# An MLP of Strassen products on one core: two pieces of the second product and two feature products in turn, in place of one and one

## The chip, the core and the metric

The kernel runs on one core of a Trainium2 chip. A core has five engines that run side by side and meet through semaphores: TensorE (PE, matmuls; PEld is its weight load), VectorE (DVE), ScalarE (ACT), GpSimd (POOL) and SyncE (SP, which here only issues DMAs). The metric is the device time of the whole program in microseconds, from its first to its last instruction, as the median over several executions.

## The reference

The program is an encoder trunk of two post-norm layers over 512 tokens of width 1024. Layer 0 mixes tokens with a gated DeltaNet, layer 1 with a gated linear attention; each is followed by the same kind of MLP, which is the part that matters here:

```python
def _sq_relu_mlp(h, w1, w2):          # h: 512 x 1024, w1: 1024 x 4096, w2: 4096 x 1024
    a = jax.nn.relu(jnp.matmul(h, w1))
    return jnp.matmul(a * a, w2)

x = _layernorm(DEEPNORM_ALPHA * x + m, ln1_g[i], ln1_b[i])                           # m: the mixer's output
x = _layernorm(DEEPNORM_ALPHA * x + _sq_relu_mlp(x, mlp_w1[i], mlp_w2[i]), ln2_g[i], ln2_b[i])
```

## The kernel before

**Three matmuls for one.** Every operand is split into a high part and the rest (`split`, line 92: a ScalarE copy, line 102, and a VectorE subtraction, line 107), and each product is the sum of high by high, high by low and low by high (`mm3`, lines 125 to 130). So all matmuls of the MLP stand on lines 128, 129 and 130, and are told apart by their tiles.

**Groups.** The MLP (`mlp`, line 352) cuts the 4096 features into four groups of 1024. For each group the first product makes the squared ReLU features `h`, and the second multiplies them by 1024 rows of w2 and adds the result to the residual `xt`. Group 0 is done with plain projections. After it, three group passes (`for gi in range(G - 1)`, line 760) each run the second product of group gi together with the feature products of group gi + 1; `last` (line 603) does the second product of group 3 with the layer norm.

**Feature products.** From group 1 on, the first product is a Strassen scheme. A group has eight feature tiles, taken as four pairs (`Pair`, line 450). A pair is made by seven half-size products (`products`, line 491): each has 4 steps of 3 matmuls, with a 128 x 128 weight and 256 moving columns, 12 in all. In order they are called A to G in this document (numbers 1, 2, 6, 5, 7, 3, 4 in the code). A, C, E and G write the PSUM tile `fx`, which accumulates over them and is copied out in between; B and then D and F write the two halves of `fyz`. The weights come from `prepare` (lines 461 to 475, run for the next pair behind D: A and B share one weight tile, D has its own) and from `late` (C and G share one tile, made behind F of the pair before; E and F share another, made behind B).

**The second product** is a Strassen scheme too (`second`, line 564): seven steps, each with four pieces (`chunks`, line 544). A piece has 2 steps of 3 matmuls with 512 moving columns, 6 in all, into one of two PSUM banks of the step; the tiles are pX, pY and pZ. A step's pieces take its two w2 tiles in turn, and for each tile both banks. With its first piece a step orders the split of the next step's operands (`upto`), with its fourth the addition of both banks to `xt` on VectorE (lines 534 and 536) and the next w2 loads. The fourth and the fifth step use the same two banks.

**The order.** 28 pieces meet 28 products in a pass. `stream` (line 740) gives the products one at a time, and between them orders the loads of the next pair (behind A) and the weights named above. The loop at lines 766 to 769 takes one piece from `second` and then as many products as `k < i + 1` allows, which is one. In the third pass (m = 24) all products that are left come behind piece 23 (the pieces count from 0), so that pieces 24 to 27 follow them. `in_order` (line 60) ties TensorE's instructions to the order in which they are written, within the block that it encloses. The other engines' order, and TensorE's between blocks, is set by the planner of the framework, from dependencies, the order of writing and its own estimates.

Of the kernel before, what the change touches and what calls it, by code (L numbers as in the profile page):

```python
# [351 lines left out]
def mlp(c, w1, w2, g, b, out=None, extra=None, room=0):  # L352
# [14 lines left out]
    with c.banks(pj=2, X=2, Y=2, Z=2), tc.tile_pool(name="mlp", bufs=2) as pool:  # L367
# [51 lines left out]
        def new_h():  # L419
            return [pool.tile([P, HF, S], F32, name="h", tag="h", bufs=3) for _ in range(2)]  # L420
# [143 lines left out]
        def second(gi, h, a):  # L564

            a11, a12, a21, a22 = quarters(h)
            tags = "ZX" if gi + 2 == G else "XZ"
            X, Y, Z = banks(tags[0]), banks("Y"), None
            load(gi, 1, 0)

            def upto(i):

                if i == 5:
                    V.tensor_tensor(a21, a22, a21, ALU.subtract)
                elif i == 6:
                    V.scalar_tensor_tensor(a11, a21, -1.0, a11, ALU.mult, ALU.subtract)
                elif i == 7:
                    V.scalar_tensor_tensor(a21, a11, -1.0, a22, ALU.mult, ALU.subtract)
                elif i == 3:
                    V.scalar_tensor_tensor(a12, a12, -1.0, a11, ALU.mult, ALU.subtract)  # L580
                b = pair({2: a12, 5: a21, 6: a11, 7: a21, 3: a12, 4: a22}[i])
                split(i)
                return b

            steps = ((1, 2, 0, 0, ALU.add, None), (2, 5, 0, 0, ALU.add, None), (5, 6, 2, 1, ALU.subtract, None),
                     (6, 7, 0, 1, ALU.subtract, (0, 0)), (7, 3, 2, 1, ALU.subtract, (0, 1)),
                     (3, 4, 0, 1, ALU.subtract, (1, 1)), (4, None, 2, 0, ALU.add, None))
            for i, nx, t, hf, op, more in steps:
                if i == 2:
                    Z = banks(tags[1])  # L590
                bk = Z if i == 2 else Y if i in (5, 3) else X
                for n, _ in enumerate(chunks(bk, a, i, i in (1, 2, 5))):
                    if n == 0 and nx:
                        b = upto(nx)
                    if n == 3:
                        for j in range(2):
                            add(t + j, hf, bk[j], op)
                        if more:
                            load(gi + 1, *more)
                    yield  # L600
                a = b
# [138 lines left out]
        def stream(gi, nh):  # L740

            for p in range(GF // 2):
                i = (gi - 1) * (GF // 2) + p
                for n, _ in enumerate(ready[i].products(nh)):
                    if n == 0:
                        begin(i + 1)
                    elif n == 1:
                        ready[i].late(1, (7, 3))
                    elif n == 3:
                        prepare(i + 1)  # L750
                    elif n == 5:
                        finish(i + 1)
                    if p == 3 and n == 2 and gi + 1 == G:
                        load(gi, 1, 0, c.wst)
                    if p == 3 and n == 2:
                        split(1, None if gi + 1 < G else True)
                        stream.a = pair(quarters(nh)[0])
                    yield

        for gi in range(G - 1):  # L760
            nh = new_h()
            more = stream(gi + 1, nh)
            n, k = 28, 0
            m = 24 if gi + 2 == G else 28
            with c.in_order(mybir.EngineType.PE):
                for i, _ in enumerate(second(gi, h, a)):
                    while k < n and (k < i + 1 or i + 1 == m):
                        next(more, None)
                        k += 1
                for _ in more:  # L770
                    pass
            h, a = nh, stream.a
# [1040 lines left out]
def body(tc, nc, a, out):  # L1813
    with contextlib.ExitStack() as es:
        def pool(name, bufs, **kw):
            return es.enter_context(tc.tile_pool(name=name, bufs=bufs, **kw))

        c = Ctx(tc, nc, (pool("const", 1), pool("big", 1), pool("wst", 3), pool("whl", 3), pool("small", 4)))
        x = a["x"][0]
        gdn(c, (a["a_in"], a["a_gates"]), a["a_conv"][0], a["a_alog"][0], a["a_dt_bias"][0], a["a_norm_g"][0],  # L1820
            a["a_out"], a["ln1_g"][0], a["ln1_b"][0], x, a["xt"], a["w1_0"])
        with tc.tile_pool(name="gcst", bufs=1) as gp:
            gc = []
            mlp(c, a["w1_0"], a["w2_0"], a["ln2_g"][0], a["ln2_b"][0],
                room=32, extra=lambda tmp: gc.append(GlaConst(c, gp, a["b_gate_b"][0], a["b_norm_g"][0], tmp)))
            gla(c, gc[0], (a["b_in"], a["b_vr"], a["b_gates"]), a["b_gate_w2"][0], a["b_out"], a["ln1_g"][1], a["ln1_b"][1], a["w1_1"])
        mlp(c, a["w1_1"], a["w2_1"], a["ln2_g"][1], a["ln2_b"][1], out=out[0])
# [18 lines left out]
```

## Time and profile before

| what | us |
|---|---|
| median of 3 executions | 1327.93 (1327.3 to 1328.49) |
| the profiled execution | 1328.52 |
| its span, first to last instruction | 1326.6 |
| TensorE busy | 1307.4 |
| VectorE busy | 1107.7 |
| ScalarE busy | 805.2 |
| pieces and products in turn, first MLP | about 466 to 701 |
| the same, second MLP | about 1040 to 1275 |

In a timeline a row has the start in us, the duration in us, the engine, the line, the operation, the tile written and the tiles read (buffer numbers left out), and the size. A matmul's duration overlaps with that of the next, so the pace of TensorE is read from the distance between starts. In a table of stretches each engine has its busy time and, after an x, the number of instructions that lie in the stretch or reach into it. In a list of waits a row says who waited for whom, how long in total, how often, and the longest.

### The profile page before, as it was taken

What the parts mean: (1) busy time and instruction counts of PE and PEld (TensorE: products, weight loads), DVE (VectorE), ACT (ScalarE), POOL (GpSimd) and SP (SyncE); (2) the same over time, 40 slices, a digit from 0 to 9 for tenths busy, and PEclk for the clock granted to TensorE, in tenths of its full rate; (3) what the DMA queues carried; (4) which work ended last, traced back from release to release, by engine and by line L of the source; (5) the groups of instructions that cost most, each with busy time, mean ns of one, the idle gap of its engine ahead of it and who ended that gap; (6) DMA issues with size and microseconds to landing.
All of it is one profiled execution on the core that took longest, in us unless ns stands there. A gap on an engine that the chain in (4) does not pass through costs nothing.

```text
span 1326.6 us, 22309 instructions
## 1 busy us (share of the span) xinstructions
PE 1307.4 (99%) x8659; PEld 1113.2 (84%) x8659; DVE 1107.7 (83%) x1823; ACT 805.2 (61%) x1598; POOL 124.8 (9%) x177
## 2 busy tenths in 40 slices
PE   9999999999999999999999999999999999999996
PEld 7777877787777889999998888888889889999985
DVE  7787888888668988989988787967879789989887
ACT  4757666767643666566667754654456466666656
POOL 5000000000000910101102200000001001101021
PEclk9999999999999999999999999999999999999998
DMA  5210120211222585675648521111216465657465
GB/s 181 96 49 33 49 65 33 64 49 57 73 99 85 189 178 154 156 191 153 151 150 170 149 90 64 65 63 64 95 64 213 105 193 154 149 172 161 142 143 143
DMA packets 44045, 154.36 MB, mean 116 GB/s; under 512 B 5419, under 2 KB 5795, under 8 KB 43939
## 3 DMA queue, kind: packets, MB, share of 16 engines
q1 hardware_dynamic: 32163, 110.85, 24.9%
q0 software_dynamic: 11776, 42.08, 16.1%
q8 instruction: 68, 1.11, 0.3%
q14 instruction: 38, 0.31, 0.1%
HBM read 113.99 MB, written 2.10 MB: 88 GB/s over the span
## 4 chain that ended last, share of the span: by engine, by line
PE 92%; ACT 3%; DVE 3%; issue 1%; DVEq 0%; POOL 0%; ACTq 0%; POOLq 0%
PE fx L128 3%; PE fx L130 3%; PE fx L129 3%; PE pX L130 3%; PE pX L129 3%; PE pX L128 3%; PE pjv L128 3%; PE pjv L129 3%; PE pjv L130 3%; PE m L1708 3%; PE fyz L128 3%; PE fyz L129 3%; PE fyz L130 3%; PE pY L129 2%; PE pY L128 2%; PE pY L130 2%
## 5 line engine op out<-in xcount | busy, mean ns | idle before, releaser
L102 ACT CAST wh<-wst 128x1024 fp32r<-128x1024 f32 x152 | 159.4, 1049 | 110.3 <-PE fyz L129 35.3
L107 DVE TENSOR_TENSOR wl<-wst,wh 128x1024 fp32r<-128x1024 f32 x150 | 184.3, 1229 | 42.2 <-ACT wh L102 41.9
L107 DVE TENSOR_TENSOR w2l<-w2r,w2h 128x1024 fp32r<-128x1024 f32 x92 | 112.3, 1221 | 24.0 <-ACT w2h L102 23.8
L102 ACT CAST w2h<-w2r 128x1024 fp32r<-128x1024 f32 x94 | 98.5, 1048 | 47.4 <-PE pX L130 16.2
L415 POOL DMA_DIRECT2D w2r<-w2r x56 | 48.5, 892 | 493.9 <-DVE w2l L107 247.3
L102 ACT CAST ah<-h 128x1024 fp32r<-128x1024 f32 x56 | 58.9, 1052 | 40.8 <-PE pX L129 18.1
L464 DVE TENSOR_TENSOR wst<-wst 128x512 f32<-128x512 f32 x120 | 79.8, 685 | 0.4
L107 DVE TENSOR_TENSOR al<-h,ah 128x1024 fp32r<-128x1024 f32 x56 | 68.3, 1220 | 5.1 <-ACT ah L102 4.8
L130 PE MATMUL pX<-w2h,al 128*128 128x512 f32 x168 | 66.2, 394 | 0.0
L129 PE MATMUL pX<-w2l,ah 128*128 128x512 f32 x168 | 66.1, 393 | 0.0
L128 PE MATMUL pX<-w2h,ah 128*128 128x512 f32 x168 | 65.8, 392 | 0.0
L128 PE MATMUL pjv<-wh,xth 128*128 128x512 f32 x128 | 54.7, 427 | 0.0
L128 PE MATMUL fx<-xth,wh 128*128 128x256 f32 x192 | 53.6, 279 | 0.0
L130 PE MATMUL fx<-xh,wl 128*128 128x256 f32 x192 | 53.6, 279 | 0.0
L130 PE MATMUL fyz<-xh,wl 128*128 128x256 f32 x192 | 53.6, 279 | 0.0
L128 PE MATMUL fyz<-xh,wh 128*128 128x256 f32 x192 | 53.6, 279 | 0.0
L128 PE MATMUL fx<-xh,wh 128*128 128x256 f32 x192 | 53.5, 278 | 0.0
L129 PE MATMUL fx<-xl,wh 128*128 128x256 f32 x192 | 53.5, 278 | 0.0
L130 PE MATMUL fx<-xth,wl 128*128 128x256 f32 x192 | 53.4, 278 | 0.0
L129 PE MATMUL fx<-xtl,wh 128*128 128x256 f32 x192 | 53.4, 278 | 0.0
L129 PE MATMUL fyz<-xl,wh 128*128 128x256 f32 x192 | 53.4, 278 | 0.0
L129 PE MATMUL pj<-xtl,wh 128*128 128x256 f32 (+1 forms) x160 | 52.0, 326 | 0.2 <-DVE xtl L194 0.2
(538 smaller groups left out, 4320.7 us busy)
## 6 DMA issues: line engine op xcount, KB each, us to landing
wst<-in_w SPq DMA_DIRECT2D x68, 512.0 KB, 4.3
w2r<-in_w SPq DMA_DIRECT2D x60, 512.0 KB, 4.0
w2r<-w2r POOLq DMA_DIRECT2D x56, 512.0 KB, 5.3
wst<-in_a_in SPq DMA_DIRECT2D x32, 512.0 KB, 3.3
wst<-in_b_vr SPq DMA_DIRECT2D x16, 512.0 KB, 3.3
wst<-in_a_out SPq DMA_DIRECT2D x8, 512.0 KB, 3.3
wst<-in_b_in SPq DMA_DIRECT2D x8, 512.0 KB, 3.3
wst<-in_b_out SPq DMA_DIRECT2D x8, 512.0 KB, 3.3
```

The lines of the kernel that those rows point to most:

```text
L102: h = nc.scalar.copy(hi, src)
L107: self.halves = h, nc.vector.tensor_tensor(lo, src, hi.bitcast(F32), ALU.subtract)
L128: mm(ps, ah, bh, start=start, stop=False, **kw)
L129: mm(ps, ah, bl, start=False, stop=False, **kw)
L130: self.last_mm = mm(ps, al, bh, start=False, stop=stop, **kw)
L415: nc.gpsimd.dma_start(blocks[a + (q,)], blocks[b + (q,)], accum_op=ALU.add)
L464: plus = lambda a, b: V.tensor_tensor(a, a, b, ALU.add)
L1708: T.matmul(ps[:, d, :], *ops(d), start=True, stop=True)
```

## The change

One condition in the loop that mixes pieces and products. Before, one product follows each piece. After, the number of products that may be out once piece i is written depends on where i stands among the seven pieces that go with a pair: behind the first, third and fifth piece it is two more, behind the seventh one, and behind the others none, so that these are followed directly by the next piece. Of one pair, with its pieces P0 to P6, the order

P0 A P1 B P2 C P3 D P4 E P5 F P6 G becomes P0 A B P1 P2 C D P3 P4 E F P5 P6 G.

The rule that all that are left come behind piece m - 1 stays.

```diff
--- before.py
+++ after.py
@@ -764,7 +764,8 @@
             m = 24 if gi + 2 == G else 28
             with c.in_order(mybir.EngineType.PE):
                 for i, _ in enumerate(second(gi, h, a)):
-                    while k < n and (k < i + 1 or i + 1 == m):
+                    upto = n if i + 1 == m else min(i + 2, 7 * (i // 7) + 7) if i % 7 in (0, 2, 4, 6) else k
+                    while k < upto:
                         next(more, None)
                         k += 1
                 for _ in more:
```

## The prediction

> **What bounds the kernel now.** I read the page's table of engines first, then the stretches of the two MLP stages (the only ones that the change touches), then the list of waits in the first of them, and last the timeline of TensorE, matmul by matmul.
>
> ```profile
> span 1326.6 us, 22309 instructions
> PE 1307.4 (99%) x8659; PEld 1113.2 (84%) x8659; DVE 1107.7 (83%) x1823; ACT 805.2 (61%) x1598; POOL 124.8 (9%) x177
> ```
>
> ```profile
> core 0: us, PE busy (x) PEld busy (x) DVE busy (x) ACT busy (x) POOL busy (x), PEclk, DMA share, GB/s
> 466.00:701.00 235.00, 235.00 (x1519) 212.28 (x1518) 207.65 (x258) 145.33 (x208) 21.75 (x26) 1.00 0.63 163
> 1040.00:1275.00 235.00, 235.00 (x1518) 212.29 (x1517) 206.45 (x254) 144.80 (x206) 20.17 (x24) 1.00 0.58 155
> ...
> 455.07:460.65 5.58, 5.58 (x25) 4.53 (x24) 5.54 (x6) 2.18 (x3) 5.17 (x7) 1.00 0.74 239
> 697.59:703.03 5.44, 5.44 (x25) 4.50 (x24) 2.90 (x4) 1.86 (x3) 0.00 (x0) 1.00 0.95 218
> ```
>
> ```profile
> PEld fx L128 <- ACT h L520: 0.4, 1, 0.4
> PEld fx L128 <- DVE h L511: 0.3, 1, 0.3
> ```
>
> The 235 us of each MLP in which products and pieces take turns are full: TensorE is busy without a break at the full granted clock (1.00), and the waits of its queue that the list shows there come to 0.7 us. VectorE is next, 207.65 of 235 us (88%). So a change of order can win only through the spacing of the matmuls themselves, and lose only through a wait that is not there now. "Busy" hides the spacing, because matmuls overlap; it is read from the starts. I call a pair's seven products A to G, and the pieces of the second product "pieces". Here are the first matmuls of products (fx, fyz: 12 matmuls of 256 columns) and pieces (pX, pY, pZ: 6 of 512) in two neighbouring pairs:
>
> ```profile
> 507.30 0.28 PE L128 MATMUL fx<-xth,wh 128*128 128x256 f32 x1
> ...
> 508.68 0.39 PE L128 MATMUL pX<-w2h,ah 128*128 128x512 f32 x1
> ...
> 510.07 0.28 PE L128 MATMUL fyz<-xth,wh 128*128 128x256 f32 x1
> ...
> 511.44 0.39 PE L128 MATMUL pX<-w2h,ah 128*128 128x512 f32 x1
> ...
> 512.83 0.28 PE L128 MATMUL fx<-xh,wh 128*128 128x256 f32 x1
> ...
> 514.25 0.39 PE L128 MATMUL pX<-w2h,ah 128*128 128x512 f32 x1
> ...
> 515.63 0.28 PE L128 MATMUL fyz<-xh,wh 128*128 128x256 f32 x1
> ...
> 517.00 0.39 PE L128 MATMUL pX<-w2h,ah 128*128 128x512 f32 x1
> ...
> 518.39 0.28 PE L128 MATMUL fx<-xh,wh 128*128 128x256 f32 x1
> ...
> 521.17 0.28 PE L128 MATMUL fyz<-xh,wh 128*128 128x256 f32 x1
> ...
> 522.57 0.39 PE L128 MATMUL pY<-w2h,ah 128*128 128x512 f32 x1
> ...
> 523.95 0.28 PE L128 MATMUL fx<-xth,wh 128*128 128x256 f32 x1
> ```
>
> ```profile
> 526.72 0.28 PE L128 MATMUL fx<-xth,wh 128*128 128x256 f32 x1
> ...
> 528.13 0.40 PE L128 MATMUL pY<-w2h,ah 128*128 128x512 f32 x1
> 529.52 0.28 PE L128 MATMUL fyz<-xth,wh 128*128 128x256 f32 x1
> ...
> 530.93 0.39 PE L128 MATMUL pY<-w2h,ah 128*128 128x512 f32 x1
> ...
> 535.12 0.28 PE L128 MATMUL fyz<-xh,wh 128*128 128x256 f32 x1
> ...
> 536.54 0.40 PE L128 MATMUL pX<-w2h,ah 128*128 128x512 f32 x1
> ...
> 540.70 0.28 PE L128 MATMUL fyz<-xh,wh 128*128 128x256 f32 x1
> ...
> 542.07 0.39 PE L128 MATMUL pX<-w2h,ah 128*128 128x512 f32 x1
> ...
> 546.23 0.28 PE L128 MATMUL fx<-xth,wh 128*128 128x256 f32 x1
> ```
>
> Two pairs, 14 products and 14 pieces, take 546.23 - 507.30 = 38.93 us. Now the same work where nothing takes turns. The window row 697.59 to 703.03 is 24 matmuls of 512 columns (x25 counts the one still running at its start): 5.44 / 24 = 0.2267 us each, so a piece of six costs 1.36 us. And at the end of the last pair, products follow each other without pieces between:
>
> ```profile
> 689.45 0.28 PE L128 MATMUL fyz<-xh,wh 128*128 128x256 f32 x1
> ...
> 690.81 0.28 PE L128 MATMUL fx<-xh,wh 128*128 128x256 f32 x1
> ```
>
> ```profile
> 1264.32 0.28 PE L128 MATMUL fyz<-xh,wh 128*128 128x256 f32 x1
> ...
> 1267.15 0.38 PE L128 MATMUL fyz<-xh,wh 128*128 128x256 f32 x1
> 1267.37 0.28 PE L129 MATMUL fyz<-xl,wh 128*128 128x256 f32 x1
> ...
> 1268.63 0.39 PE L128 MATMUL pX<-w2h,ah 128*128 128x512 f32 x1
> ```
>
> The first is product D right behind C: 690.81 - 689.45 = 1.36 us for 12. At these rates the two pairs would take 28 x 1.36 = 38.08 us; they take 0.85 us more, 0.061 us for each product with its piece. That excess is all that the change can win.
>
> **The change part by part.** It removes, adds and resizes no instruction. Of each seven pieces (P0 to P6) and products the order P0 A P1 B P2 C P3 D P4 E P5 F P6 G becomes P0 A B P1 P2 C D P3 P4 E F P5 P6 G: P1, P3 and P5 each change places with the product behind them. Per MLP that is 12 exchanges in each of the first two group passes and 10 in the third (P23 is followed by C to G in both orders), 34; 68 in all, or 68 / 3 = 22.7 pairs' worth.
>
> *Matmul spacing.* After the change P2, P4 and P6 stand second of two pieces, and B, D and F second of two products.
>
> Second pieces: P2, P4 and P6 are the pieces whose end is the start of C, E and G. The rows give 1.39 (511.44 to 512.83), 1.39 (517.00 to 518.39) and 1.38 us (522.57 to 523.95). A piece that follows pieces costs 1.36. I take 1.365, as a little of the settling may reach over: a gain of 0.022 to 0.025, three times, 0.07 us a pair. The ends are 0 and 0.09.
>
> D: now 1.37 (515.63 to 517.00) in one pair and 1.42 (535.12 to 536.54) in the next, mean 1.395; behind C it took 1.36. Gain 0.03.
>
> F: now 1.40 (521.17 to 522.57) and 1.37 (540.70 to 542.07), mean 1.385. In the tail it follows E from 1267.15 to 1268.63, 1.48 us, of which its first step (0.22 us against 0.11) holds 0.11 of waiting: 1.37. Gain 0.015.
>
> B behind A is nowhere in the trace. B goes on in the weight tile and the x tile that A reads, so it should keep A's spacing, and A takes 1.38 in the one pair (507.30 to 508.68) and 1.41 in the other (526.72 to 528.13); B now takes 1.37 and 1.41. I take 0.005 as the gain; the ends are -0.02 (all at 1.41) and 0.03 (all at 1.36).
>
> A, C, E and G keep the same predecessor and are taken at no change. For the bounds they could all come to 1.36 (C, 512.83 to 514.25, takes 1.42 now) or to 1.41: with the others, about 0.3 us a pair won or 0.13 lost, 7 us or 3 us in all.
>
> Sum: 0.07 + 0.03 + 0.015 + 0.005 = 0.12 us a pair; times 22.7 = 2.7 us.
>
> [...]
>
> *Waits.* No wait is added, but B, D and F start 1.38 us sooner and P1, P3 and P5 as much later. I went through what each needs. B uses A's weights. D needs a weight tile of its own, made ready in the pair before; F uses E's weights, and E keeps its time. In PSUM, every product that adds to a bank which ScalarE or VectorE has copied out (C after A, D after B, E after C, F after D, G after E) has two pieces and one product between, before and after: 2 x 1.39 + 1.38 = 4.2 us. The tail shows what it costs without that cover: with E alone between D and F, F's first step takes 0.11 us more. DMA issues keep their order on SyncE's and GpSimd's queues: a pair's loads follow its A, the second product's loads follow a step's fourth piece, and no exchange passes the one by the other. I cost all of it at nothing; the cover is those 4.2 us, and VectorE's 12% of free time.
>
> The tightest place is where two steps of the second product in a row use the same banks (counted through the pass from 0, P14 and P15 end the one, P16 and P17 open the next; here P15 starts at 508.68, P16 at 511.44). P16 writes the bank that P14 ended, and VectorE must have added it to xt before.
>
> ```profile
> 508.20 1.22 DVE L107 TENSOR_TENSOR wl<-wst,wh 128x1024 fp32r<-128x1024 f32 x1
> 509.34 0.68 DVE L534 SCALAR_TENSOR_TENSOR xt<-xt,pX 128x512 f32<-128x512 f32 x1
> 510.26 0.69 DVE L534 SCALAR_TENSOR_TENSOR xt<-xt,pX 128x512 f32<-128x512 f32 x1 [0.25 <-PE pX L130]
> ```
>
> The row at 509.34 is that addition (P14 ended at 507.30); it is over at 510.02, which leaves 1.4 us. In the new order P16 stands directly behind P15, with A and B ahead of both, so it starts at the same time: the 1.4 us stay, provided VectorE keeps its order.
>
> **The rivals.**
>
> *All of the excess goes with the turns.* Then each removed pair of turns saves the whole 0.061 us: 68 x 0.061 = 4.1 us, 1323.8. For it: D loses its 1.42 when it stands behind C. Against: C needs 1.42 in a stretch where A, in the same position, needs 1.38, so part of the spacing belongs to the tiles.
>
> *The spacing belongs to the tiles, not to the order.* The window 455.07 to 460.65, plain features with no turns at all, has 24 matmuls of 512 in 5.58 us, 0.2325 each, as slow as any piece that takes turns. If that is the rule, the change does nothing: 1327.9. Against: pieces behind pieces at 1.36 within the very same tiles. [...]
>
> *VectorE's order turns against it (the slower side).* Everything but TensorE is ordered by a planner from its own estimates, and P1, P3, P5 come later for it. If two more subtractions of 1.22 us, like the row at 508.20, get ahead of the addition at 509.34, it ends 2.44 us later and P16 waits 2.44 - 1.4 = 1.0 us. There is one such place in each of three passes of two MLPs: 6 us, less the 2.7 won: 1331.2. It decides from 1.4 us of delay on. For it: VectorE is at 88%. Against: the waits of TensorE come to 0.7 us in 235, and neither P14 nor P16 moves.
>
> **How the numbers follow.** The profiled execution took 1328.52 us, 1.9 over its span of 1326.6 and 0.6 over the median of 1327.93; the change lies within the span, so it goes off the median: 1327.93 - 2.7 = 1325.2. What a measurement of this kernel can tell from no change is about 0.2%, 2.66 us, which is nearly the forecast itself. Chances: the forecast 0.60 (its own range 1323.5 to 1326.9; 0.35 of it beyond 0.2%, 0.25 within), all of the excess 0.14 (faster), the tiles alone 0.16 (no change), VectorE's order or slower spacing throughout 0.10 (slower). Together: faster 0.49, same 0.41, slower 0.10. The range takes in the first rival and a part of the bounds above (7 us won, 3 lost), and leaves out the ends: 1322.4 to 1329.0.
>
> **What would show it.** Right: pieces in second place 1.36 to 1.37 us apart by their starts, D at 1.36 in every pair, two pairs at 38.93 - 0.24 = 38.7 us, the list of waits under 1 us for TensorE. Wrong: A, C, E or G moved by more than 0.03 us each (the bounds of the firsts), pieces in second place still at 1.39 (tiles alone), or a wait of TensorE for an addition to xt (VectorE's order).

## The result, and the profile after

| | before | after |
|---|---|---|
| median, us | 1327.96 | 1344.68 |
| ratio, 95% interval | 1 | 1.0127 [1.0109, 1.0144] |
| profiled span, us | 1326.6 | 1343.5 |

The change makes the kernel 16.7 us slower; the forecast was 2.7 us faster. From the page of the changed kernel:

```profile
span 1343.5 us, 22356 instructions
PE 1313.5 (98%) x8659; PEld 1117.8 (83%) x8659; DVE 1109.8 (83%) x1823; ACT 808.9 (60%) x1598; POOL 125.7 (9%) x177
```

The same number of matmuls, and the same busy times but for TensorE, which is now busy for 6 us more and still idle for 11 us more than before (1343.5 - 1313.5 = 30.0 against 1326.6 - 1307.4 = 19.2). The list of waits of TensorE and of its weight loads in the first MLP's turns (466 to 707) has one entry each; before, it had 0.7 us in all:

```profile
PE fx L128 <- DVE h L511: 5.9, 3, 2.0
```

```profile
PEld fx L128 <- DVE h L511: 7.4, 4, 2.4
```

Line 511 is VectorE's addition of product E to `h`; it frees the bank `fx` for product G. There are three long waits per MLP, one per pass, each in the first pair of the pass. This is the first one, in the timeline of TensorE (F, P5, P6, G):

```profile
480.33 0.28 PE L128 MATMUL fyz<-xh,wh 128*128 128x256 f32 x1
...
481.70 0.39 PE L128 MATMUL pZ<-w2h,ah 128*128 128x512 f32 x1
...
483.09 0.39 PE L128 MATMUL pZ<-w2h,ah 128*128 128x512 f32 x1
...
484.24 0.39 PE L130 MATMUL pZ<-w2h,al 128*128 128x512 f32 x1
486.58 0.39 PE L128 MATMUL fx<-xth,wh 128*128 128x256 f32 x1 [1.95 <-DVE h L511]
```

E is over when F starts, at 480.33. F, P5 and P6 run, as forecast, and at the spacing of the pieces G would start 0.23 us behind P6's last matmul, at 484.47. It starts at 486.58, 2.1 us late. What VectorE did meanwhile, in its own timeline:

```profile
477.36 1.23 DVE L107 TENSOR_TENSOR wl<-wst,wh 128x1024 fp32r<-128x1024 f32 x1 [0.81 <-ACT wh L102]
478.50 0.68 DVE L534 SCALAR_TENSOR_TENSOR xt<-xt,pX 128x512 f32<-128x512 f32 x1
479.10 0.68 DVE L464 TENSOR_TENSOR wst<-wst 128x512 f32<-128x512 f32 x1
479.70 1.22 DVE L107 TENSOR_TENSOR al<-h,ah 128x1024 fp32r<-128x1024 f32 x1
480.83 1.28 DVE L464 TENSOR_TENSOR wst<-wst 128x512 f32<-128x512 f32 x2
482.04 1.21 DVE L107 TENSOR_TENSOR w2l<-w2r,w2h 128x1024 fp32r<-128x1024 f32 x1
483.18 0.68 DVE L471 TENSOR_TENSOR wl<-wst,wh 128x512 fp32r<-128x512 f32 x1
483.78 1.28 DVE L464 TENSOR_TENSOR wst<-wst 128x512 f32<-128x512 f32 x2
484.98 1.21 DVE L107 TENSOR_TENSOR w2l<-w2r,w2h 128x1024 fp32r<-128x1024 f32 x1
486.12 0.41 DVE L511 TENSOR_TENSOR h<-h,fx 128x256 f32<-128x256 f32 x1
```

In this stretch VectorE never idles from 477.36 on, and E's addition stands last. Ahead of it are the weights of the next pair (`prepare`: the first `wl`, five sums on line 464, line 471) and the three subtractions of the next step (`al`, two `w2l`). In the kernel before, in the same pair, the addition ran in the middle of that work:

```profile
479.85 1.22 DVE L107 TENSOR_TENSOR wl<-wst,wh 128x1024 fp32r<-128x1024 f32 x1
480.99 1.22 DVE L578 SCALAR_TENSOR_TENSOR h<-h 128x1024 f32<-128x1024 f32 x1
482.12 0.69 DVE L464 TENSOR_TENSOR wst<-wst 128x512 f32<-128x512 f32 x1
482.73 0.41 DVE L511 TENSOR_TENSOR h<-h,fx 128x256 f32<-128x256 f32 x1
483.06 1.29 DVE L464 TENSOR_TENSOR wst<-wst 128x512 f32<-128x512 f32 x2
```

G started there at 484.85, so that 1.7 us were left between the end of the addition (483.14) and G:

```profile
484.85 0.28 PE L128 MATMUL fx<-xth,wh 128*128 128x256 f32 x1
```

In the kernel before, the first `wl` of the next pair came at 479.85, 2.5 us later. What it waits for is the weight tile that product D gives back, by the row of its ScalarE copy in the changed kernel:

```profile
476.27 1.05 ACT L102 CAST wh<-wst 128x1024 fp32r<-128x1024 f32 x1 [0.89 <-PE fyz L129]
```

So the chain reads: D ends a piece sooner, `prepare` may begin sooner, and the planner's order of VectorE now has all of that work ahead of E's addition. Not all of it was ready earlier. The copy for line 471 had to wait for product F:

```profile
481.82 0.62 ACT L470 CAST wh<-wst 128x512 fp32r<-128x512 f32 x1 [2.27 <-PE fyz L129]
```

E was over at 480.33 and F at 481.70. So the addition stood behind work that became ready after it; the order of the queue held it, and not a lack of readiness.

A second cost follows the wait. Behind the wait in the second pass, the table of stretches of the changed kernel (stretch, its length, TensorE busy with the number of instructions, granted clock, DMA share, GB/s) shows the clock at half:

```profile
566.71:569.84 3.13, 3.13 (x15) 0.51 0.94 178
```

Adding up how far each step from one start to the next exceeds 0.113 us (256 columns) or 0.227 us (512), over the turns of both MLPs, the six long waits are 12.7 us, the half-clock steps and short waits 7.5 us (1.1 before), and the ordinary spacing 1.2 us less than before: 12.7 + 6.4 - 1.2 = 17.9 us. What lies ahead of the turns and behind them gives back 1.0, and the span grew by 16.9.

### The profile page after: what moved, and what is told of

It reads as the page before. It is cut to its first block, busy times and chain, and to the rows that moved or that the text cites. A ratio compares the mean times of both kernels' runs of the same rounds, so it can differ in the third digit from the quotient of the medians.

```text
span 1343.5 us, 22356 instructions
## 1 busy us (share of the span) xinstructions
PE 1313.5 (98%) x8659; PEld 1117.8 (83%) x8659; DVE 1109.8 (83%) x1823; ACT 808.9 (60%) x1598; POOL 125.7 (9%) x177
```

## The experiments

**Where it happens.** The new order, but the first pair of each pass keeps one and one:

```diff
+ upto = n if i + 1 == m else i + 1 if i < 7 else min(i + 2, 7 * (i // 7) + 7) if i % 7 in (0, 2, 4, 6) else k
```

> The new order everywhere but in the first pair of each pass, which keeps one and one. Theory (VectorE queue): in the new order D ends a piece sooner, frees the weight tile sooner, and the next pair's weight work (prepare) and the next step's subtractions, all written ahead of E's addition, are ready before E is and fill VectorE; only in the first pair of a pass do both kinds meet ahead of E. Then all six stalls of 2.1 us are gone with this edit, and what is left is the gain of spacing, which the trace of the changed kernel puts at about 0.5 us per MLP: 1327.0 to 1327.5. Rival (every pair's E is near the edge, the first pair is only the first to show it): stalls move to the second pair, three per MLP, 1335 or more.

Measured: 1327.22 us against 1327.55, ratio 0.9995 [0.9987, 1.0004]. No step of the turns is more than 0.16 us late, and the time is as the theory said. The loss sits in the first pairs alone, and the rest of the new order is worth too little to tell from no change.

**The order of writing.** TensorE's order as in the change, `prepare` written behind E instead of behind D, in all pairs:

```diff
-                    elif n == 3:
+                    elif n == 4:
                         prepare(i + 1)
```

> The new order of TensorE untouched; prepare(i + 1) is written behind product E instead of behind D, so E's addition stands ahead of it in the program. Theory: the addition gets ahead of prepare's seven VectorE operations, G no longer waits, TensorE's clock stays full, and the time is that of before less about 1 us of spacing: 1326.5 to 1327.5. Rival (the subtraction of the second w2 tile, which waits for piece P5, holds up the addition, not prepare): G still waits about 1 to 2 us in six places, 1335 to 1345. A third possibility: the next pair's weights now come late and A or D waits instead.

Measured: 1328.67 us, ratio 1.0007 [0.9998, 1.0016], over the 1327.5 expected at most. The six waits are gone, which speaks for the theory and against the rival, for the second `w2l` still waits for P5. The third possibility came true as well, in a small way: B waits 0.8 to 0.9 us once per MLP in a later pair, which the trace puts down to ScalarE's work on the product G before it (line 520).

**One exchange at a time.** D with P3 alone:

```diff
+ upto = n if i + 1 == m else i + 1 + (i % 7 == 2)
```

> Only D is exchanged with P3 (P0 A P1 B P2 C D P3 P4 E P5 F P6 G); B and F stay as before. Theory (D's earlier end makes prepare's work ready before E is): the six stalls are here, 1.5 to 2.5 us each, with the half clock behind some of them: 1337 to 1346. Rival (P5's later end makes the second w2 subtraction late, and the addition stands behind it): P5 is where it was, no stall, 1327 to 1328.

Measured: 1335.68 us, ratio 1.0055 [1.0042, 1.0069]. Six waits in the same places, of 1.47 to 1.51 us, at full clock; both the waits and the time are at or just under the least expected (1.5 us, 1337). TensorE's list of waits in the first MLP:

```profile
PE fx L128 <- DVE h L511: 3.9, 3, 1.3
```

B and F exchanged, D as before:

```diff
+ upto = n if i + 1 == m else i + 1 + (i % 7 in (0, 4))
```

> Only B is exchanged with P1 and F with P5 (P0 A B P1 P2 C P3 D P4 E F P5 P6 G); D stays as before. Theory (D's earlier end is the cause): no stall, 1327 to 1328. Rival (P5's later end is the cause): the six stalls are here, 1335 to 1345.

Measured: 1329.19 us, ratio 1.0009 [1.0, 1.0018], a little over the 1328 expected. There is none of the six waits, but one of 0.74 us per MLP in the fourth pair of the first pass, again for E's addition, which the theory had not foreseen:

```profile
543.02 0.38 PE L128 MATMUL fx<-xth,wh 128*128 128x256 f32 x1 [0.58 <-DVE h L511]
```

So the long waits come with D's exchange. That E's addition has little room elsewhere too is the part of the rival of the first run that holds. An exchange moves two things, though: D ends sooner, and P3, the last piece of its step, ends later; ScalarE's copy `ah` for the next step starts at 477.55 in the changed kernel and at 476.49 before. No run moves one without the other. What the runs show is that writing `prepare` behind E is enough to take the waits away with P3 left where it is.

D and F exchanged, B as before, and then B and D exchanged, F as before:

```diff
+ upto = n if i + 1 == m else i + 1 + (i % 7 in (2, 4))
```

```diff
+ upto = n if i + 1 == m else i + 1 + (i % 7 in (0, 2))
```

> D and F exchanged, B as before (P0 A P1 B P2 C D P3 P4 E F P5 P6 G). Theory (D's exchange makes the stall of 1.5 us, and F's exchange, which puts P5 later and with it the second w2 subtraction, adds 0.6): six stalls of 2.1 us, four or so with the half clock behind them: 1342 to 1346. Rival (B's exchange adds the 0.6): six of 1.5 us at full clock, 1334 to 1337.

> B and D exchanged, F as before (P0 A B P1 P2 C D P3 P4 E P5 F P6 G). Theory: six stalls of 1.5 us, full clock behind them, as with D alone: 1334 to 1337. Rival (B's exchange adds the 0.6 us): six of 2.1 us with the half clock, 1342 to 1346.

Measured: D and F 1346.45 us, ratio 1.0139 [1.0125, 1.0153], six waits of 2.12 us; B and D 1334.86 us, ratio 1.0052 [1.0039, 1.0066], six waits of 1.47 to 1.51 us. Both came as the theory said, but for a time 0.45 us above the 1346 given for D and F. So D's exchange makes 1.5 us of the wait, F's adds 0.6 once D is exchanged, and B's nothing. With D alone, VectorE's timeline has the second `w2l` in the middle of the queue, the addition at 484.35, and one sum behind the addition:

```profile
482.01 0.68 DVE L464 TENSOR_TENSOR wst<-wst 128x512 f32<-128x512 f32 x1
482.61 1.22 DVE L107 TENSOR_TENSOR w2l<-w2r,w2h 128x1024 fp32r<-128x1024 f32 x1
483.75 0.68 DVE L471 TENSOR_TENSOR wl<-wst,wh 128x512 fp32r<-128x512 f32 x1
484.35 0.41 DVE L511 TENSOR_TENSOR h<-h,fx 128x256 f32<-128x256 f32 x1
484.68 0.68 DVE L464 TENSOR_TENSOR wst<-wst 128x512 f32<-128x512 f32 x1
```

With all three exchanged the second `w2l` stands at 484.98, right ahead of the addition and behind all five sums. The fifth sum, 0.60 us from start to start, is the 0.6 us. Why it got ahead is not separated: F's exchange puts P5 later, and the second `w2l` with it, as the theory has it, but it also ends F sooner, for which the copy on line 470 waits, and with it line 471 and the last two sums.

**The length of the queue.** The change, with two of the five sums of the pair in question left out:

```diff
-                plus(t0[:, h:, :], t0[:, :h, :])
+                if self.p != 1:
+                    plus(t0[:, h:, :], t0[:, :h, :])
...
-                plus(t0[:, h:, :], t1[:, h:, :])
+                if self.p != 1:
+                    plus(t0[:, h:, :], t1[:, h:, :])
```

> The changed kernel, with two of the five weight sums (line 464) of the second pair of each pass left out; the features of that pair are therefore computed from incomplete weight sums. Theory (E's addition waits behind a queue of VectorE work that is already there): each sum left out ahead of it moves it up by 0.6 us, so the six stalls shrink from 2.1 to about 0.9 us and TensorE keeps its full clock behind them: 1344.7 - 6 x 1.2 - about 6 of half clock = 1331 to 1332. Rival (the addition is held by the second w2 subtraction, which itself waits for P5 and its ScalarE copy, not by the length of the queue): that one still ends at the earliest 1.2 us behind its copy, and the stalls stay at 1.5 us or more: 1335 or more.

Measured: 1325.27 us, ratio 0.9982 [0.9973, 0.9991] (with work left out, so no gain to be had). Neither number came: the waits are gone, not shortened. VectorE's timeline says why (lines below 468 stand one or two further down in this kernel; 513 is E's addition):

```profile
480.07 1.21 DVE L107 TENSOR_TENSOR w2l<-w2r,w2h 128x1024 fp32r<-128x1024 f32 x1
481.21 0.68 DVE L472 TENSOR_TENSOR wl<-wst,wh 128x512 fp32r<-128x512 f32 x1
481.81 0.41 DVE L513 TENSOR_TENSOR h<-h,fx 128x256 f32<-128x256 f32 x1
482.14 0.68 DVE L464 TENSOR_TENSOR wst<-wst 128x512 f32<-128x512 f32 x1
...
483.08 1.22 DVE L107 TENSOR_TENSOR w2l<-w2r,w2h 128x1024 fp32r<-128x1024 f32 x1
```

The planner placed the addition ahead of one sum and of the second `w2l`. The queue decides, but through an order that is made anew for each kernel; the delay cannot be had by subtracting durations from the old order. So this run does not tell the theory from its rival either, as the second `w2l` moved too. Which of the planner's estimates tips the order was not tried and stays open.

**A version without the wait.** The change, with `prepare` written behind E in the first pair of a pass only:

```diff
-                    elif n == 3:
+                    elif n == (4 if p == 0 else 3):
                         prepare(i + 1)
```

> The new order throughout; prepare is written behind E in the first pair of a pass only, behind D elsewhere. Theory: the first pair is the only place where prepare and the next step's subtractions meet ahead of E's addition, and the 0.8 us that B waited in some passes with prepare behind E everywhere belonged to other pairs: no stall over 0.2 us in the turns, 1326.0 to 1327.0, under both kernels by about 1 us. Rival (the order of writing in other pairs is thrown by this too): single waits of about 0.8 us, 1328 to 1329.

Measured: 1326.46 us against 1327.75, ratio 0.9991 [0.9983, 1.0000]: the time as forecast, and a gain that the interval just fails to tell from none. The addition now stands ahead of `prepare`'s sums:

```profile
479.44 1.22 DVE L107 TENSOR_TENSOR w2l<-w2r,w2h 128x1024 fp32r<-128x1024 f32 x1
480.57 0.41 DVE L511 TENSOR_TENSOR h<-h,fx 128x256 f32<-128x256 f32 x1
480.91 0.68 DVE L464 TENSOR_TENSOR wst<-wst 128x512 f32<-128x512 f32 x1
```

One wait over 0.2 us is left (B, 0.36 us in the second MLP). TensorE's order is that of the change here, and only the place of `prepare` in the writing differs: from 1344.68 us it takes back the whole loss. That shows the order on VectorE to be the cause.

The same writing, with only B and D exchanged:

> B and D exchanged, F as before, and prepare behind E in the first pair of a pass. In the traces so far a pair takes 19.40 us on the mean with B and D exchanged, 19.42 with all three, 19.46 with none (pairs without a stall). Theory: the writing behind E takes the stalls away here too, and the spacing gives 22 x 0.06 = 1.3 us: 1326.0 to 1326.5, level with or just under the run with all three exchanged. Rival: another order of the planner, with waits of 0.3 to 0.9 us here and there: 1327 to 1328.

Measured: 1325.18 us against 1327.93, ratio 0.9979 [0.9970, 0.9988], the lowest of the kernels that leave nothing out, and 0.8 us under the least expected. No step in the turns is more than 0.13 us late, and a pair takes 19.37 or 19.44 us in turn (19.42 and 19.51 before, by the starts of the pairs' first products).

## Why the prediction was wrong, step by step

**What bounds the kernel** held: TensorE back to back, with VectorE next. "Lose only through a wait that is not there now" is what happened.

**Waits: the step that failed.** "I cost all of it at nothing; the cover is those 4.2 us, and VectorE's 12% of free time." The 4.2 us between E and G are there, F, P5 and P6 without a gap. But they cover a single VectorE operation only if it runs when it is ready. It waited 5.8 us (480.33 to 486.12) behind other work. The prediction asked what B, D and F need, and not what their earlier end sets free: D gives a weight tile back, and the first of the seven VectorE operations of `prepare` waits for it, the others behind that one. In place of nothing, the waits cost 12.7 us, and the half clock and short waits that came with them 6.4. The 12% of free time is a mean; from 477.36 to 486.53 there was none.

The kernel before showed how little of the cover was free. The prediction worked out the room of the addition to `xt` (1.4 us), but not that of E's addition, which was 1.7 us in the first pair and not 4.2. The list of waits that it shows even had one for line 511, of 0.3 us.

**The rival on the slower side** had the mechanism, VectorE's order, and the wrong place: P16 and the addition to `xt`, which stayed where they were. It priced 6 places at 1.0 us. There were 6, at 2.1 us, and behind four of them TensorE's granted clock fell to 0.50, which no step of the prediction had. That its count of places came out is luck: it counted other places.

**Spacing** had the right sign and was too large: two pairs without a wait take 38.85 us after the change (508.94 to 547.79) against 38.93, a gain of 0.08 and not of 0.24. From the starts in the changed kernel, in a pair without a wait:

```profile
508.94 0.28 PE L128 MATMUL fx<-xth,wh 128*128 128x256 f32 x1
...
510.35 0.28 PE L128 MATMUL fyz<-xth,wh 128*128 128x256 f32 x1
...
511.71 0.39 PE L128 MATMUL pX<-w2h,ah 128*128 128x512 f32 x1
...
513.09 0.39 PE L128 MATMUL pX<-w2h,ah 128*128 128x512 f32 x1
...
514.46 0.28 PE L128 MATMUL fx<-xh,wh 128*128 128x256 f32 x1
...
515.87 0.28 PE L128 MATMUL fyz<-xh,wh 128*128 128x256 f32 x1
...
517.26 0.39 PE L128 MATMUL pX<-w2h,ah 128*128 128x512 f32 x1
...
518.65 0.39 PE L128 MATMUL pX<-w2h,ah 128*128 128x512 f32 x1
...
520.03 0.28 PE L128 MATMUL fx<-xh,wh 128*128 128x256 f32 x1
...
521.39 0.28 PE L128 MATMUL fyz<-xh,wh 128*128 128x256 f32 x1
...
522.76 0.39 PE L128 MATMUL pX<-w2h,ah 128*128 128x512 f32 x1
...
524.15 0.39 PE L128 MATMUL pY<-w2h,ah 128*128 128x512 f32 x1
...
525.53 0.28 PE L128 MATMUL fx<-xth,wh 128*128 128x256 f32 x1
...
526.95 0.39 PE L128 MATMUL pY<-w2h,ah 128*128 128x512 f32 x1
...
528.35 0.28 PE L128 MATMUL fx<-xth,wh 128*128 128x256 f32 x1
...
547.79 0.28 PE L128 MATMUL fx<-xth,wh 128*128 128x256 f32 x1
```

Of the second pieces, P2 takes 1.37 (513.09 to 514.46), but P4 and P6 take 1.38 (518.65 to 520.03, 524.15 to 525.53), where 1.365 was taken for all three; P6 gained nothing. That is about half of the 0.07 forecast. D behind C takes 1.39 (515.87 to 517.26) and not the 1.36 of the tail. F at 1.37 (521.39 to 522.76) came as forecast, and B at 1.36 here.

"A, C, E and G are taken at no change" failed as well: G now takes 1.42 (525.53 to 526.95) in place of 1.38, and A 1.41 (508.94 to 510.35) in place of 1.38, while E won (1.36 in place of 1.39). G moved by more than the 0.03 that the prediction named as a sign of being wrong. G's loss belongs to F's exchange: in the run with B and D exchanged and `prepare` behind E in the first pair, where F stays, G takes 1.38. Why some products and pieces take longer than others in the same place is not shown by any run.

The range ended at 1329.0. It left out that one wait per pass can cost several times the gain. A bound would have reached there: 8.8 us of VectorE's work ran ahead of E's addition without a gap (477.36 to 486.12), which is 4.6 more than the 4.2 us of cover. The same kinds of operation take as long in the trace of the kernel before (a subtraction 1.22 us, a sum 0.69, E's addition 0.41). With six places that allows some 28 us of loss, an estimate from these rows.

## What to carry to other kernels

When an order is changed on a full engine, look not only at what each moved piece needs but at what its earlier end sets free: buffers that come back sooner let other engines' work begin sooner (here the first `wl`, at 477.36 and not at 479.85), and a queue whose order is fixed beforehand may then run that work ahead of the short operation on which the full engine depends (here for 5.8 us). Here it helped to write the operation that frees an accumulator ahead of preparation for later, in the one place where both came together. An average of free time on the second engine is no cover for one late operation (here 12% stood beside a wait of 2.1 us); look at the room that this operation itself has in the trace.

## What the runs showed of the hardware

Behind waits of 2.1 us TensorE's granted clock fell in some cases and not in others. The changed kernel has six of them in the turns. Behind four the clock fell to 0.50, 0.3 to 1.4 us after the wait was over (566.49, 647.96, 1070.56 and 1231.86), and stood there for 3.41 us:

```profile
566.80:570.21 3.41, 3.41 (x15) 0.50 1.01 190
648.72:652.13 3.41, 3.41 (x13) 0.50 0.92 172
1071.97:1075.38 3.41, 3.41 (x13) 0.50 1.00 189
1232.40:1235.81 3.41, 3.41 (x14) 0.50 0.93 175
```

In the first of these stretches the products' matmuls start 0.21 to 0.22 us apart, where 0.113 is usual. Behind the other two waits, over at 486.58 and 1152.02, the clock stayed full:

```profile
486.58:490.58 4.00, 4.00 (x28) 1.00 0.96 179
1152.02:1156.02 4.00, 4.00 (x28) 1.00 0.96 180
```

What sets these two apart from the four, the runs do not settle. With D and F exchanged, which gives six waits of the same length, the mean granted clock of the four executions was 0.991 to 0.993, as in the changed kernel (0.992 and 0.993) and under the 0.996 or 0.997 of the kernel before; behind the first wait the stretch 487.50:490.50 has 0.60.

The waits of 1.5 us were not followed by it. With D alone both stretches that hold the six waits (466 to 700, 1045 to 1278) have a clock of 1.00, and with B and D exchanged the mean of each execution was 0.997, against 0.996 or 0.997 in the kernel before. The window behind the first of the waits, with D alone:

```profile
484.81:487.50 2.69, 2.69 (x18) 1.00 1.02 192
```
